# Hybrid encoder layer on one core: output block products with another order of splits and reads, row statistics on ScalarE, and an earlier sum for the last attention block

## The chip, the cores and the metric

The kernel runs on one core of a Trainium2 chip. The metric is the device time of one execution in microseconds (us), and the figure for a kernel is the median of several executions. "Faster" and "slower" mean a smaller and a larger median.

Five engines work side by side, each with a queue of its own that it takes strictly in order: PE (TensorE, the matrix multiplications), DVE (VectorE), ACT (ScalarE), POOL (GpSimd) and SP (SyncE, which here only issues DMAs). An engine waits when the next instruction in its queue needs a result of another engine or of a DMA; everything behind that instruction waits with it.

## The reference

One layer of a bidirectional encoder for 2048 tokens of width 1024, in float32. Two groups of heads work on the same input, their results stand side by side, one projection mixes them, and a LayerNorm closes the layer:

```python
def hybrid_mixer(x, positions, w_in, ..., w_out):
    h = x @ w_in
    (g_q, g_k, g_v, g_gate, g_lr_f, g_lr_b, m_cq, m_ckv, m_kr, m_gate) = jnp.split(h, idx, axis=-1)
    o_a = gla_branch(g_q, g_k, g_v, g_gate, g_lr_f, g_lr_b, ...)        # gated linear attention, width 512
    o_b = mla_branch(m_cq, m_ckv, m_kr, m_gate, positions, ...)         # latent attention, softmax, width 512
    return jnp.concatenate([o_a, o_b], axis=-1) @ w_out

def layer_norm(t, g, b):
    mu = jnp.mean(t, axis=-1, keepdims=True)
    var = jnp.mean(jnp.square(t - mu), axis=-1, keepdims=True)
    return (t - mu) * lax.rsqrt(var + LN_EPS) * g + b

x = layer_norm(DEEPNORM_ALPHA * x + mixed, ln_g, ln_b)
```

The change touches the end only: the last block of the softmax attention, the product with `w_out`, and the LayerNorm of its rows.

## The kernel before

**Stages.** Input projection and gated linear attention come first, then 16 blocks of softmax attention (one head and 512 queries each), then the product with `w_out`. The last two overlap; the stretch that matters here is the last 125 us of 1291.

**Precision by three matmuls.** Every float32 operand is split into a part `hi` (rounded, by ACT, line 392) and the rest `lo` (by POOL or DVE, line 398). One product is three matmuls, hi·hi, hi·lo and lo·hi, recorded at lines 446, 447 and 448 (`mm3`). So the matmul of line 448 is the first one that needs the `lo` part of the left operand.

**Output product, chunks 0 to 7.** The 2048 rows are 16 chunks of 128. Chunks 0 to 7 are multiplied directly: `product` or `part` issues 24 matmuls for each of the two halves of 512 columns. `residual` adds ALPHA times the input rows and takes row statistics of each half on DVE (`bn_stats`, line 2241). `finish_a` joins the statistics (line 2253 `mv`, line 2254 `u`), subtracts the mean and multiplies with `ln_g` (line 2256, two halves), and has ACT work out 1/sqrt in six small instructions (lines 2258 to 2263, `ln_l` to `ln_r`). `finish_b` multiplies with that and adds `ln_b` (line 2269, two halves on DVE), and SP writes the rows out (line 2270). `ln_psum` (line 2144) copies `ln_g` and `ln_b` into PSUM early in this stage.

**Output product, chunks 8 to 15.** Two chunks at a time form a `Pair` (line 1961), four pairs in all. Row 0 of pair p is chunk 9+2p, row 1 is chunk 8+2p. A pair is a 2x2 block product after Strassen and Winograd: seven products P1 to P7 of half size, 12 matmuls each, in place of eight. The left operands are A11, A12, A22 and the sums S1 to S4 (`add`, DVE line 2008). The seven products go in turn to four PSUM banks `pw0` to `pw3`, and each bank is used again within the pair and by the next pair. What empties the banks: ACT copies bank 0 twice (`c1`, `c7`, line 2033), DVE adds these copies into bank 2 (`U2`, `U3`, line 2036), and DVE reads the banks into the output rows (line 2042 for the first read of a half, line 2044 for later ones; R1, R5, R5b, R6, R2, R7 belong to row 0 or to both, R3, R4, R4b to row 1). The half rows get their statistics at line 2050.

**What feeds a pair.** `load` (line 1974) has SP fetch the two inputs of a chunk and its gates; `gate` (line 1996) has POOL multiply half of the chunk with two gates, two instructions for each chunk. The tiles that pairs 1 and 3 load into are named `lng` and `lnb` in the trace, since they are the slots that ln_g and ln_b came in; those of pairs 0 and 2 are named `of`.

**What sets the order.** In this last stage each instruction gets a place, a time in us: that of the pair plus a number of the table `PLACE_PAIR` (lines 140 to 148). All are sorted by place and `in_order` (line 408) ties them in that order on every engine. The numbers give an order alone; when a thing runs is decided by its waits.

**The last attention block.** Its row sums are turned and added by `tsum` (four small transposes on PE, `sx15`), then `rcp` on DVE (a reduction, line 1762, and a reciprocal, line 1766). `turn` transposes the reciprocals on PE (`rt`, line 1777), `y` multiplies the block with its value weights on PE (tile `y`), and `yc` copies that out on ACT (line 1806). The bank that `y` uses is the one that the first half of chunk 7 (`po7`) is written to next.

Of the kernel before, what the change touches and what calls it, by code (L numbers as in the profile page):

```python
# [9 lines left out]
F32 = mybir.dt.float32  # L10
# [133 lines left out]
    read=dict(c1=2.78, R1=5.99, R5=7.88, U2=10.61, R6=11.24, R5b=11.87, R2=12.5, bn12=13.13, c7=14.91, U3=15.63,  # L144
              R3=16.26, bn22=16.89, R7=17.52, bn11=18.15, R4=20.34, R4b=20.97, bn21=21.6, fa=(18.78, 22.23), fb=(23.79, 25.68)),
    read_last=dict(c1=2.78, R1=5.99, R5=7.88, U2=10.61, R6=11.24, R5b=11.87, R2=12.5, bn12=13.13, R7=13.7, bn11=14.3, c7=16.4,
                   U3=17.1, R3=17.7, bn22=17.8, R4b=17.71, fa=(14.9, 20.0), fb=(17.9, 24.0)),
# [234 lines left out]
class K:  # L382
# [1215 lines left out]
    def attention(self):  # L1598
# [4 lines left out]
        with ExitStack() as ctx:  # L1603
# [357 lines left out]
class Pair:  # L1961
# [76 lines left out]
    def read(self, r, n, ps, first, cs=slice(0, 512)):  # L2038
        o = self.rows[r]
        rr = o["rr"][:, n, cs]  # L2040
        if first:
            self.nc.vector.scalar_tensor_tensor(rr, o["xr"][:, n, cs], ALPHA, ps(), ALU.mult, ALU.add)
        else:
            self.nc.vector.tensor_tensor(rr, ps(), rr, ALU.add)
# [6 lines left out]

    def put(self, put, T, last):
# [23 lines left out]
        at(e["c7"], self.copy, bank[b["P7"]])  # L2076
        at(e["U3"], self.sum, bank[2])
        for n, r, h, x, first in (("R1", 0, 0, 0, True), ("R5", 1, 1, 1, True), ("R6", 0, 1, 3, True), ("R5b", 0, 1, 1, False),
                                  ("R2", 0, 1, 2, False), ("R3", 1, 1, 2, False), ("R7", 0, 0, b["P2"], False),
                                  ("R4b", 1, 0, 2, last)) + (() if last else (("R4", 1, 0, 3, True),)):  # L2080
            at(e[n], self.read, r, h, bank[x], first)
        at(e["bn12"], self.stats, 0, 1, 1)
        at(e["bn11"], self.stats, 0, 0, 0)
        if not last:
            at(e["bn22"], self.stats, 1, 1, 1)
            at(e["bn21"], self.stats, 1, 0, 0)
        else:
            at(e["bn22"], self.stats, 1, 1, 2, 3)
            for i, x in enumerate((3, 0)):
                cs, half = slice(256 * i, 256 * i + 256), lambda x=x: bank[x]()[:, :256]  # L2090
                at(t["P4"] + PAIR_US / 14 * i, self.product, "P4", half, cs)
                at(t["P4"] + PAIR_US / 14 * (i + 1) + 0.05, self.read, 1, 0, half, False, cs)
                at(t["P4"] + PAIR_US / 14 * (i + 1) + 0.06, self.stats, 1, 0, i, 3, cs)
        for r in range(2):
            at(e["fa"][r], op.finish_a, self.rows[r])
            at(e["fb"][r], op.finish_b, self.rows[r])


class OutProj:
# [147 lines left out]
    def finish_a(self, o):  # L2247
        kern, nc, sm = self.k, self.nc, self.sm
        V, Ac = nc.vector, nc.scalar
# [5 lines left out]
        for n in range(2):  # L2255
            V.scalar_tensor_tensor(rr[:, n], rr[:, n], mv[:, 0:1], self.ln[0][n], ALU.subtract, ALU.mult)
        l, y, t, w, rs = (sm.tile([P, 1], F32, tag=f"rs_{i}", name=f"ln{c}_{i}") for i in "lytwr")
# [8 lines left out]
    def finish_b(self, o):  # L2266
        kern, nc, c, rr = self.k, self.nc, o["c"], o["rr"]
        for n in range(2):
            nc.vector.scalar_tensor_tensor(rr[:, n], rr[:, n], o["rs"], self.ln[1][n], ALU.mult, ALU.add)
# [69 lines left out]
```

## Time and profile before

| what | value |
|---|---|
| median of three executions | 1294.27 us (1293.17, 1294.27, 1297.21) |
| the profiled execution, its own time | 1292.98 us |
| the profiled execution, its span in the trace | 1291.2 us |
| mean granted clock of TensorE | 0.994 |
| PE busy | 1258.6 us, 97% of the span |
| DVE busy | 955.1 us, 74% |
| ACT busy | 862.1 us, 67% |
| POOL busy | 845.4 us, 65% |
| chunk 7's last product ends, pair 0 begins | 1198.4 us |
| first matmul of pairs 1, 2 and 3 | 1221.9, 1240.9 and 1261.1 us |
| last matmul | 1280.3 us |

Times within the trace count from the start of the span. A row of the timeline gives the start, the duration, the engine, the line, the operation, the tile written and the tiles read, the shape, and in square brackets how long the engine had been idle before it and what it had waited for. Matmul starts are 0.227 us apart at the full clock for the usual 128x512 tile; the record's own duration is longer since matmuls overlap.

### The profile page before, as it was taken

To read this page: it belongs to the slowest core of one execution; us is meant where nothing else is said; L and a number is where in the kernel's file an instruction comes from. 1 tells how busy PE (TensorE), PEld (TensorE's weight loads), DVE (VectorE), ACT (ScalarE), POOL (GpSimd) and SP (SyncE) were. 2 spreads that over 40 slices of the span, in tenths; PEclk is the share of its full clock that TensorE was granted. 3 is DMA by queue.
4 is the path that set the end of the run, shared out by engine and by line. 5 is a ranking of instruction groups with operands and counts; after the bars stand their busy time and mean duration, and the time that the engine had idled before them with its cause. 6 is when DMAs were issued, how large, how long until landed. Compare 5 with 4: busy or idle time off the path is not lost.

```text
span 1291.2 us, 20146 instructions
## 1 busy us (share of the span) xinstructions
PE 1258.6 (97%) x6928; PEld 1112.4 (86%) x6928; DVE 955.1 (74%) x1722; ACT 862.1 (67%) x1520; POOL 845.4 (65%) x544
## 2 busy tenths in 40 slices
PE   7999999999999999999999999999999999999996
PEld 7999999999889999999788888888888888887775
DVE  6865775555675555555898888888888889468898
ACT  7765657666676556655688888888888888523432
POOL 0245555453567666671288888889999999946861
PEclk9999999999999999999999999999999999999998
DMA  8332525253665555565401111122223112368851
GB/s 296 96 93 62 181 69 171 82 156 98 221 218 182 189 193 180 196 213 167 135 1 41 42 41 41 42 58 66 58 79 101 42 41 103 127 217 321 284 196 65
DMA packets 122518, 166.81 MB, mean 129 GB/s; under 512 B 18502, under 2 KB 71118, under 8 KB 121776
## 3 DMA queue, kind: packets, MB, share of 16 engines
q1 hardware_dynamic: 114256, 163.39, 39.7%
q0 software_dynamic: 768, 2.10, 0.5%
q8 instruction: 55, 0.90, 0.3%
q10 hardware_dynamic: 7392, 0.03, 0.3%
q14 instruction: 47, 0.39, 0.2%
HBM read 106.72 MB, written 58.75 MB: 128 GB/s over the span
## 4 chain that ended last, share of the span: by engine, by line
PE 76%; DVE 6%; POOL 4%; DMA 3%; ACT 3%; issue 3%; SPq 1%; DVEq 0%; POOLq 0%; ACTq 0%
PE pS L1632 4%; PE pS L1634 4%; PE pS L1635 4%; PE pS L1633 4%; PE pS L1636 4%; PE o L446 4%; PE o L447 4%; PE o L448 4%; PE ipa L446 3%; PE ipa L448 3%; PE ipa L447 3%; PE pz L447 2%; PE pz L446 2%; PE pz L448 2%; PE ipg L446 2%
## 5 line engine op out<-in xcount | busy, mean ns | idle before, releaser
L398 POOL TENSOR_TENSOR pl<-s,ph 128x1024 fp32r<-128x1024 f32 x128 | 306.1, 2415 | 56.3 <-ACT ph L392 56.3
L1654 DVE TENSOR_TENSOR rm<-pS,rm 128x512 f32<-128x512 f32 x210 | 144.8, 689 | 26.2 <-ACT s L1641 20.6
L1678 DVE TENSOR_TENSOR s<-s,mb 128x1024 f32<-128x1024 f32 x128 | 151.2, 1213 | 9.4 <-PE mb L1672 9.3
L1641 ACT ACTIVATE s<-pS 128x1024 f32<-128x1024 f32 x128 | 131.2, 1025 | 37.5 <-PE pS L1636 33.4
L392 ACT ACTIVATE ph<-s 128x1024 fp32r<-128x1024 f32 x128 | 134.9, 1057 | 13.5 <-PE o L448 12.7
L1682 ACT ACTIVATE s<-s 128x1024 f32<-128x1024 f32 x128 | 131.5, 1051 | 13.4 <-DVE s L1678 13.3
L446 PE MATMUL ipa<-wah,xah 128*128 128x384 f32 (+1 forms) x384 | 130.5, 340 | 6.7 <-ACT wah L392 6.7
L1095 POOL TENSOR_TENSOR Us<-Us,cw 128x512 f32<-128x512 f32 x16 | 18.6, 1163 | 174.1 <-DVE Us L1093 158.6
L448 PE MATMUL ipa<-wah,xal 128*128 128x384 f32 (+1 forms) x384 | 125.3, 326 | 0.0
L447 PE MATMUL ipa<-wal,xah 128*128 128x384 f32 (+1 forms) x384 | 125.0, 326 | 0.0
L1632 PE MATMUL pS<-qh,ckvT_h 128*128 128x512 f32 x256 | 102.7, 401 | 0.8 <-DVE rm L1654 0.4
L446 PE MATMUL o<-ph,vh 128*128 128x512 f32 x256 | 101.2, 395 | 0.0
L1633 PE MATMUL pS<-ql,ckvT_h 128*128 128x512 f32 x256 | 99.9, 390 | 0.0
L1635 PE MATMUL pS<-rh,krs 128*128 128x512 f32 x256 | 99.9, 390 | 0.0
L1634 PE MATMUL pS<-qh,ckvT_l 128*128 128x512 f32 x256 | 99.9, 390 | 0.0
L448 PE MATMUL o<-ph,vl 128*128 128x512 f32 x256 | 99.9, 390 | 0.0
L1636 PE MATMUL pS<-rl,krs 128*128 128x512 f32 x256 | 99.9, 390 | 0.0
L447 PE MATMUL o<-pl,vh 128*128 128x512 f32 x256 | 99.8, 390 | 0.0
L1705 DVE TENSOR_TENSOR ap<-ap,s 128x512 f32<-128x512 f32 x120 | 83.1, 692 | 3.5 <-ACT s L1682 0.9
L446 PEld LDWEIGHTS ipa<-wah,xah 128*128 128x128 f32 x384 | 73.6, 192 | 7.2 <-ACT wah L392 6.7
L446 PE MATMUL pz<-xch,wzh 128*128 128x256 f32 x256 | 74.9, 293 | 0.0
L447 PEld LDWEIGHTS ipa<-wal,xah 128*128 128x128 f32 x384 | 73.6, 192 | 0.6 <-DVE wal L398 0.2
(433 smaller groups left out, 3901.0 us busy)
## 6 DMA issues: line engine op xcount, KB each, us to landing
xcf<-xT_dram SPq DMA_DIRECT2D x16, 512.0 KB, 5.1
xr<-x_dram SPq DMA_DIRECT2D x16, 512.0 KB, 6.3
xaf<-xT_dram SPq DMA_DIRECT2D x14, 512.0 KB, 3.9
wb<-wO_dram SPq DMA_DIRECT2D x16, 256.0 KB, 2.9
oib<-oi_s SPq DMA_DIRECT2D x16, 256.0 KB, 4.0
qdb<-qd_s SPq DMA_DIRECT2D x16, 256.0 KB, 4.4
SU<-su_s SPq DMA_DIRECT2D x16, 256.0 KB, 4.7
ub<-u_s SPq DMA_DIRECT2D x16, 256.0 KB, 4.2
```

Of the source, the lines that this page charges most:

```text
L392: return nc.scalar.activation(dst, src, AF.Copy).ins
L398: return e.tensor_tensor(dst, src, hi.bitcast(F32), ALU.subtract).ins
L446: mm(out, ah, bh, start=start, stop=False)
L447: mm(out, ah, bl, start=False, stop=False)
L448: mm(out, al, bh, start=False, stop=stop)
L1632: mm(ps[:, e], kh, qh, start=True, stop=False)
L1633: mm(ps[:, e], kh, ql, start=False, stop=False)
L1634: mm(ps[:, e], kl, qh, start=False, stop=False)
L1635: mm(ps[:, e], kr, rh, start=False, stop=False)
L1636: mm(ps[:, e], kr, rl, start=False, stop=True)
L1654: V.tensor_tensor(d["rm"], src[:, e], d["rm"], ALU.max)
L1678: V.tensor_tensor(s, s, d["mb"][:, None, :].to_broadcast([P, 2, QB]), ALU.subtract)
```

## The change

Five things, all in the last 125 us.

1. For the last attention block, `tsum` and `rcp` are issued before the product of chunk 5 and no longer after it.
2. On POOL the `lo` part of S4 of pair 0 moves up from the place 4.49 to -2.2, which is ahead of the gates of pair 1. Those gates get places of their own (`gate1`).
3. In pairs 0 to 2 the banks are read in another order: R5b directly after R5, R2 ahead of R6. Row 0 no longer gets its statistics from `bn_stats` on DVE but from ACT: `squares` sums the row by a copy of 128x1024 that accumulates, makes the negative mean `nm`, and squares the two halves with the mean taken off, accumulating again; `scale` makes the variance and runs the six instructions of 1/sqrt. On DVE `centre` subtracts the mean and multiplies with `ln_g` in one instruction of 128x1024. The places of `finish_a` and `finish_b` move. On SP the write of xr8 moves behind the four loads of chunk 15.
4. In the last pair the second copy (`c7`) and U3 are gone; DVE reads P7's bank itself for the two halves of row 1 that need it (R3p, R4p), two more reads. `copy_lnb` has ACT copy `ln_b` from PSUM to SBUF. Row 0 of the last pair is finished by ACT (scale) and POOL (add of that copy) in place of DVE (`finish_first`).
5. `ln` becomes a tile of 128x2x512 in place of a list of halves, and the 1/sqrt chain a function (`rsqrt`) of its own.

```diff
-    read=dict(c1=2.78, R1=5.99, R5=7.88, U2=10.61, R6=11.24, R5b=11.87, R2=12.5, bn12=13.13, c7=14.91, U3=15.63,
-              R3=16.26, bn22=16.89, R7=17.52, bn11=18.15, R4=20.34, R4b=20.97, bn21=21.6, fa=(18.78, 22.23), fb=(23.79, 25.68)),
-    read_last=dict(...),
+    gate1=((-14.6, -13.3), (-19.95, -18.6)),
+    read=dict(c1=2.78, R1=5.9, R5=6.5, R5b=7.1, U2=10.61, R2=11.24, R6=11.87, c7=14.91, U3=15.63, R3=16.26, bn22=16.89,
+              R7=17.52, sq=18.25, R4=20.34, R4b=20.97, bn21=21.6, rs=21.9, fa=(21.7, 22.23), fb=(23.9, 26.7)),
+    read_last=dict(c1=2.78, lnb=3.5, R1=5.0, R5=6.3, R5b=6.9, U2=8.9, R2=9.5, R3=10.1, R4b=10.7, R6=11.5, bn12=12.1,
+                   R7=14.1, bn11=14.7, R3p=16.9, R4p=17.5, bn22=18.1, fa=(15.3, 20.2), fb=(17.0, 20.3)),
...
+                    if c > 4:
+                        tsum(nb - 1)
+                        rcp(nb - 1)
                     op.product(rest[c])
                     op.finish(rest[c])
-                with self.after(*last.values()), fixed():
-                    for f in {4: (tot, oh, ol), 5: (tsum, rcp)}[c]:
-                        f(nb - 1)
+                if c == 4:
+                    with self.after(*last.values()), fixed():
+                        for f in (tot, oh, ol):
+                            f(nb - 1)
...
+    def squares(self, r):
+        Ac, o = self.nc.scalar, self.rows[r]
+        t, o["nm"] = self.small(o, "st"), self.small(o, "nm")
+        o["sq"] = [self.small(o, f"sq{n}") for n in range(2)]
+        Ac.activation(o["rr"], o["rr"], AF.Copy, accum_out=t)
+        Ac.activation(o["nm"], t, AF.Copy, scale=-1.0 / D)
+        for n, tag in enumerate(("wv_h", "wv_l")):
+            q = self.op.bp.tile([P, QB], F32, tag=tag, name=f"{tag}q{o["c"]}", bufs=1)
+            Ac.activation(q, o["rr"][:, n], AF.Square, bias=o["nm"], accum_out=o["sq"][n])
+
+    def scale(self, r):
+        Ac, o = self.nc.scalar, self.rows[r]
+        v, u = self.small(o, "v"), self.small(o, "u")
+        Ac.activation(v, o["sq"][1], AF.Copy, scale=1.0 / D, bias=LN_EPS)
+        Ac.activation(u, o["sq"][0], AF.Identity, scale=1.0 / D, bias=v)
+        self.op.rsqrt(o, u)
+
+    def centre(self, r):
+        o = self.rows[r]
+        self.nc.vector.scalar_tensor_tensor(o["rr"], o["rr"], o["nm"], self.op.ln[0], ALU.add, ALU.mult)
+
+    def copy_lnb(self):
+        self.lnb = self.op.bp.tile([P, 2, 512], F32, tag="pl", name="lnbc", bufs=3)
+        self.nc.scalar.activation(self.lnb, self.op.ln[1], AF.Copy)
+
+    def finish_first(self):
+        o, c = self.rows[0], self.c[0]
+        for n in range(2):
+            rr = o["rr"][:, n]
+            self.nc.scalar.activation(rr, rr, AF.Copy, scale=o["rs"])
+            self.nc.gpsimd.tensor_tensor(rr, rr, self.lnb[:, n], ALU.add)
+            self.nc.sync.dma_start(self.k.out[c * P:(c + 1) * P, n * 512:(n + 1) * 512], rr)
...
-                at(P_["gate"][r][n], self.gate, r, n)
+                at(P_["gate1" if self.p == 1 else "gate"][r][n], self.gate, r, n)
...
-            at(P_["lo"][n], self.lo, n)
+            at(-2.2 if n == "S4" and not self.p else P_["lo"][n], self.lo, n)
...
+        if last:
+            reads = (("R1", 0, 0, 0), ("R5", 1, 1, 1), ("R5b", 0, 1, 1), ("R2", 0, 1, 2), ("R3", 1, 1, 2), ("R4b", 1, 0, 2),
+                     ("R6", 0, 1, 3), ("R7", 0, 0, b["P2"]), ("R3p", 1, 1, b["P7"]), ("R4p", 1, 0, b["P7"]))
```

The table's numbers show little by themselves, so three places follow as the instructions stand in the queues.

**DVE, around the sums of the last attention block.** The row of line 1762 adds the sums (`sx`, from PE) and that of line 1766 takes their reciprocal. `rr_12919` is chunk 4, `rr_13042` and `rr_13050` are chunk 5. Before:

```order
L2253 BN_AGGR mv_12949<-bn_12920 128x2
L2254 TENSOR_SCALAR u_12950<-mv_12949 128x1
L2256 SCALAR_TENSOR_TENSOR rr_12919<-rr_12919,mv_12949,lng 128x512 x2
L2269 SCALAR_TENSOR_TENSOR rr_12919<-rr_12919,ln_r,lnb 128x512 x2
L398 TENSOR_TENSOR ofl_12974<-o_12437,ofh_12972 128x512
L2240 SCALAR_TENSOR_TENSOR rr_13042<-xr_12818,po_12993 128x512 x2
L2241 BN_STATS bn_13043<-rr_13042 128x6 x2
L1762 TENSOR_REDUCE rc_13074<-sx_13069 128x4
L2253 BN_AGGR mv_13048<-bn_13043 128x2
L1766 RECIPROCAL rc_13074<-rc_13074 128x4
```

With the change:

```order
L1763 TENSOR_REDUCE rc_12998<-sx_12993 128x4
L2308 BN_AGGR mv_12949<-bn_12920 128x2
L1767 RECIPROCAL rc_12998<-rc_12998 128x4
L2309 TENSOR_SCALAR u_12950<-mv_12949 128x1
L2311 SCALAR_TENSOR_TENSOR rr_12919<-rr_12919,mv_12949,lng 128x512 x2
L2328 SCALAR_TENSOR_TENSOR rr_12919<-rr_12919,ln_r,lnb 128x512 x2
L399 TENSOR_TENSOR ofl_12974<-o_12437,ofh_12972 128x512
L2295 SCALAR_TENSOR_TENSOR rr_13050<-xr_12818,po_13001 128x512 x2
```

The reduction and the reciprocal moved from behind chunk 5's statistics to ahead of chunk 4's finish. On PE the four transposes moved likewise, from behind chunk 5's 48 matmuls to ahead of them. (Line numbers of the changed kernel are higher by 1 at line 398 and by up to 60 further down.)

**POOL, between pair 0 and pair 1.** Line 398 makes `lo` parts, line 1996 applies gates; `lng` and `lnb` are the chunks of pair 1 here. Before:

```order
L398 TENSOR_TENSOR S2l_13228<-of_12988,S2h_13224 128x512
L1996 TENSOR_TENSOR lnb<-lnb,gr_12729 128x512
L398 TENSOR_TENSOR S3l_13264<-of_12888,S3h_13261 128x512
L1996 TENSOR_TENSOR lnb<-lnb,gr_12729 128x512
L1996 TENSOR_TENSOR lng<-lng,gr_12739 128x512 x2
L398 TENSOR_TENSOR A22l_13320<-of_12888,A22h_13268 128x512
L398 TENSOR_TENSOR A12l_13338<-of_12988,A12h_13259 128x512
L398 TENSOR_TENSOR S4l_13344<-of_12988,S4h_13266 128x512
L398 TENSOR_TENSOR A11l_13358<-lng,A11h_13322 128x512
```

With the change:

```order
L399 TENSOR_TENSOR S2l_13228<-of_12988,S2h_13224 128x512
L399 TENSOR_TENSOR S3l_13263<-of_12888,S3h_13260 128x512
L399 TENSOR_TENSOR S4l_13269<-of_12988,S4h_13265 128x512
L2001 TENSOR_TENSOR lnb<-lnb,gr_12729 128x512 x2
L399 TENSOR_TENSOR A22l_13320<-of_12888,A22h_13267 128x512
L399 TENSOR_TENSOR A12l_13338<-of_12988,A12h_13258 128x512
L2001 TENSOR_TENSOR lng<-lng,gr_12739 128x512 x2
L399 TENSOR_TENSOR A11l_13359<-lng,A11h_13322 128x512
```

S4's `lo` part of pair 0 now stands ahead of six instructions that it stood behind: the four gates of pair 1, A22l and A12l. The number of instructions up to A11l of pair 1 is the same.

**DVE, where the last pair begins.** `xr_13589` is row 0 of pair 2 (chunk 13), `xr_13612` row 1 (chunk 12), `xr_13783` and `xr_13806` are the rows of the last pair (chunks 15 and 14). With the change:

```order
L2081 SCALAR_TENSOR_TENSOR xr_13589<-xr_13589,nm_13855,ln_13112 128x1024
L2308 BN_AGGR mv_13913<-bn_13851 128x2
L2309 TENSOR_SCALAR u_13914<-mv_13913 128x1
L2311 SCALAR_TENSOR_TENSOR xr_13612<-xr_13612,mv_13913,ln_13112 128x512 x2
L2328 SCALAR_TENSOR_TENSOR xr_13589<-xr_13589,ln_r,ln_13115 128x512 x2
L2048 SCALAR_TENSOR_TENSOR xr_13783<-xr_13783,pw_13272 128x512
L2048 SCALAR_TENSOR_TENSOR xr_13806<-xr_13806,pw_13273 128x512
L2048 SCALAR_TENSOR_TENSOR xr_13783<-xr_13783,pw_13273 128x512
L2328 SCALAR_TENSOR_TENSOR xr_13612<-xr_13612,ln_r,ln_13115 128x512 x2
L2041 TENSOR_TENSOR pw_13274<-pw_13274,pc_13894 128x512
L2050 TENSOR_TENSOR xr_13783<-pw_13274,xr_13783 128x512
L2050 TENSOR_TENSOR xr_13806<-pw_13274,xr_13806 128x512
```

The finish of chunk 13 (line 2328, first of the two) stands ahead of all reads of the last pair, as it did before; the centring ahead of it is one instruction, and after it three first reads stand together. On ACT, `lnbc` (the copy of `ln_b`) stands behind the 1/sqrt chains of chunks 13 and 12, and in the program the finish of chunk 13 waits for it, since both read the same PSUM tile.

More of the change, by code (lines that the diff above doesn't have):

```diff
@@ L2075, in put @@
         at(e["U2"], self.sum, bank[2])
[L2076 to L2083, printed above, removed]
+        if last:
+            reads = (("R1", 0, 0, 0), ("R5", 1, 1, 1), ("R5b", 0, 1, 1), ("R2", 0, 1, 2), ("R3", 1, 1, 2), ("R4b", 1, 0, 2),
+                     ("R6", 0, 1, 3), ("R7", 0, 0, b["P2"]), ("R3p", 1, 1, b["P7"]), ("R4p", 1, 0, b["P7"]))
+        else:
+            at(e["c7"], self.copy, bank[b["P7"]])
+            at(e["U3"], self.sum, bank[2])
+            reads = (("R1", 0, 0, 0), ("R5", 1, 1, 1), ("R5b", 0, 1, 1), ("R2", 0, 1, 2), ("R6", 0, 1, 3), ("R3", 1, 1, 2),
+                     ("R7", 0, 0, b["P2"]), ("R4", 1, 0, 3), ("R4b", 1, 0, 2))
+        for n, r, h, x in reads:
+            at(e[n], self.read, r, h, bank[x])
         if not last:
@@ L2135, in load_ln @@
             self.nc.sync.dma_start(t, self.k.ins[n].rearrange("p (a d) -> p a d", a=2))
-        self.ln = [[t[:, n] for n in range(2)] for t in self.ln_sb]
+        self.ln = list(self.ln_sb)
     def pair_banks(self):
@@ L2144, in ln_psum @@
         self.nc.scalar.activation(t, self.ln_sb[w], AF.Copy)
-        self.ln[w] = [t[:, n] for n in range(2)]
+        self.ln[w] = t
     def fetch_t(self, n):
```

52 lines of the change are left out of this document (33 added, 19 removed).

## The prediction

> **What bounds the kernel now.** I read the share of busy time first (PE 97%), then PE's own waits in the last 190 us, since whatever PE does not wait for cannot be won there. The view of waits, from 1100 us on (engine, line, releaser: total us, times, longest):
>
> ```profile
> PE rt L1777 <- DVE u L2254: 2.6, 1, 2.6
> PE pw L448 <- POOL S4l L398: 2.5, 1, 2.5
> PE pw L446 <- DVE xr L2044: 0.8, 1, 0.8
> ```
>
> Three stalls, and the change aims at all of them. What a stall really costs is in the windows (PE, PEld, DVE, ACT, POOL busy, then granted clock, DMA share, GB/s):
>
> ```profile
> 1210.00:1214.00 4.00, 4.00 (x12) 3.17 (x11) 2.90 (x3) 1.33 (x3) 2.71 (x3) 0.59 1.07 364
> 1240.00:1260.00 20.00, 19.19 (x85) 15.57 (x84) 19.45 (x32) 8.05 (x21) 12.69 (x11) 1.00 0.38 143
> ```
>
> After the 2.5-us stall the clock is 0.59 for one stretch; after the 0.8-us stall (1255.5) it stays 1.00. The second row also shows DVE as good as full (19.45 of 20) while PE has 0.8 to spare: in the pairs DVE paces. Now PE's timeline at the first stall and at the pairs' first matmuls:
>
> ```profile
> 1176.74 0.39 PE L448 MATMUL pmb<-woh,ol 128*128 128x512 f32 x1
> 1179.68 0.27 PE L1777 MATMUL rt<-ident,rc 128*4 128x128 f32 x1 [2.56 <-DVE u L2254]
> 1180.87 0.63 PE L446 MATMUL px<-woh,oh 128*128 128x512 f32 x1
> 1183.42 0.41 PE L446 MATMUL px<-woh,oh 128*128 128x512 f32 x1
> 1187.53 0.39 PE L446 MATMUL po<-woh,oh 128*128 128x512 f32 x1
> 1198.41 0.39 PE L446 MATMUL pw<-woh,A11h 128*128 128x512 f32 x1
> 1221.86 0.39 PE L446 MATMUL pw<-woh,A11h 128*128 128x512 f32 x1
> 1240.90 0.39 PE L446 MATMUL pw<-woh,A11h 128*128 128x512 f32 x1
> 1261.07 0.39 PE L446 MATMUL pw<-woh,A11h 128*128 128x512 f32 x1
> ```
>
> From 1180.87 to 1183.42 six matmuls take 2.55 us, 0.425 each against 0.227 later: with `rt` and `y` about eight slow ones, some 1.6 us on top of 2.56. A pair without a stall takes 84 matmuls, 84 x 0.227 = 19.05 us (pair 1: 1240.90 - 1221.86 = 19.04). Pair 0 took 23.45, 4.4 too much: 2.5 waiting, 1.9 slow. Pair 2 took 20.17, 1.1 too much.
>
> The Trainium skill, "TensorE: Matmul & The Clock Gate", Part 1, has it that the clock drops after at least one idle window of about 3.4 us and that the slow stretch lasts as long. Here idle times of 2.46 and 2.56 us sufficed, and the slow stretch agrees (1180.0 to 1183.4). By that number neither stall would have slowed PE, and taking away the one at S4l would win 2.5 us where the rows give 4.4; the rows decide.
>
> **First part: the sums one chunk sooner.** `rt` waits for DVE's reciprocal, which stands behind chunk 5's statistics:
>
> ```profile
> 1178.65 0.67 DVE L1762 TENSOR_REDUCE rc<-sx 128x4 f32<-128x512 f32 x1
> 1179.36 0.18 DVE L1766 RECIPROCAL rc<-rc 128x4 f32<-128x4 f32 x1
> 1185.46 0.63 ACT L392 ACTIVATE A11h<-of 128x512 fp32r<-128x512 f32 x1 [1.92 <-DMA of<-oa_s]
> 1186.15 0.57 ACT L1806 ACTIVATE yc<-y 128x512 f32<-128x512 f32 x1
> ```
>
> Placed ahead of chunk 4's finish the reciprocal is done some 9 us earlier, so `rt` follows at 1177.1 without a wait: 2.56 + 1.6 = 4.2 us off this place. But the next thing behind is `po`, which writes the bank that `yc` copies out, and `yc` stands on ACT behind A11h, which waits for its input until 1185.46. `yc` ends at 1186.72 whatever PE does. PE, ready at 1187.53 - 4.2 = 1183.3, would idle to 1186.8: 3.5 us, longer than the two stalls that dropped the clock, so another 1.6 us slow. Pair 0 then starts at 1198.41 - 0.73 + 1.6 = 1199.25, 0.85 later than before; without a clock drop 0.75 sooner. I take the drop. So this part by itself wins nothing; it swaps one stall for another.
>
> **Second part: S4's lo part.** POOL and the wait's other end:
>
> ```profile
> 1198.50 0.63 ACT L392 ACTIVATE S4h<-of 128x512 fp32r<-128x512 f32 x1 [1.15 <-DVE of L2008]
> 1199.82 1.29 POOL L398 TENSOR_TENSOR S3l<-of,S3h 128x512 fp32r<-128x512 f32 x1
> 1207.89 1.71 POOL L398 TENSOR_TENSOR S4l<-of,S4h 128x512 fp32r<-128x512 f32 x1
> 1216.93 1.29 POOL L1996 TENSOR_TENSOR of<-of,gr 128x512 f32<-128x512 f32 x1 [2.27 <-DMA of<-ob_s]
> 1225.81 1.31 POOL L398 TENSOR_TENSOR S4l<-lng,S4h 128x512 fp32r<-128x512 f32 x1
> ```
>
> S4h is there at 1199.1. In the new order POOL makes S4l right behind S3l, which no longer waits for a gate: done near 1200.5 instead of 1209.6, while P3 of pair 0 asks for it at 1199.25 + 8.16 + 0.45 = 1207.9. Stall and slow stretch go: -4.4. What it is moved past (four gates, A22l, A12l) has slack: at 1.27 us each A12l is done near 1205.5, wanted at 1212.9; pair 1's A11l ends near 1209.3, as before. SP's next load waits for A22l, but also stands behind a write that sets its time (the write of chunk 7), so it is not moved. Pair 1 starts at 1199.25 + 19.05 = 1218.3 instead of 1221.86: -3.56.
>
> **What is late next.** The gates of pair 2 stand on POOL ahead of pair 1's S4l. The gate at 1216.93 waited for a DMA, and from it on POOL works without a gap: S4l of pair 1 ends at 1227.1, as before. P3 of pair 1 now asks for it at 1218.3 + 8.61 = 1226.9. A wait of 0.2: the pace has reached the transfer. This is a floor: pair 2 cannot start before 1237.6 (before: 1240.90, so -3.3), and it hardly matters whether pair 0 came 0.85 later or 0.75 sooner.
>
> **Third part: DVE relieved in the pairs.** The first read after the old pair's centring, three pairs in a row, and ahead of the last one the end of a pair:
>
> ```profile
> 1222.43 0.68 DVE L2042 SCALAR_TENSOR_TENSOR xr<-xr,pw 128x512 f32<-128x512 f32 x1
> ...
> 1242.61 0.68 DVE L2042 SCALAR_TENSOR_TENSOR xr<-xr,pw 128x512 f32<-128x512 f32 x1
> ...
> 1260.15 0.69 DVE L2050 BATCH_NORM_STATS2 bn<-xr 128x6 f32<-128x512 f32 x1
> 1260.88 0.21 DVE L2253 BATCH_NORM_AGGREGATE mv<-bn 128x2 f32<-128x12 f32 x1
> 1261.12 0.15 DVE L2254 TENSOR_SCALAR u<-mv 128x1 f32<-128x1 f32 x1
> 1261.19 1.40 DVE L2256 SCALAR_TENSOR_TENSOR xr<-xr,mv,ln 128x512 f32<-128x512 f32 x2
> 1262.51 0.68 DVE L2042 SCALAR_TENSOR_TENSOR xr<-xr,pw 128x512 f32<-128x512 f32 x1
> ```
>
> From read to read (1222.43, 1242.61, 1262.51) DVE needs 20.2 and 19.9 us. Two `bn_stats` (0.73 to the next start here, some 0.61 elsewhere) and row 0's `mv` and `u` (0.24, 0.07) go: -1.65. What moves to ACT, and a wider form on DVE, have these nearest rows:
>
> ```profile
> L1678 DVE TENSOR_TENSOR s<-s,mb 128x1024 f32<-128x1024 f32 x128 | 151.2, 1213 | 9.4 <-PE mb L1672 9.3
> L1682 ACT ACTIVATE s<-s 128x1024 f32<-128x1024 f32 x128 | 131.5, 1051 | 13.4 <-DVE s L1678 13.3
> L1379 ACT ACTIVATION_READ_ACCUMULATOR sqm<-ipm x16: 186/194/195, 376.3 to 592.8; 128x1 f32 x16
> L1540 ACT ACTIVATE og<-Ob x16: 578/595/599, 381.3 to 586.5; 128x512 f32<-128x512 f32 x16
> 1276.80 0.20 ACT L2258 ACTIVATE ln_l<-u 128x1 f32<-128x1 f32 x1 [10.04 <-DVE u L2254]
> 1278.36 0.58 ACT L2033 ACTIVATE pc<-pw 128x512 f32<-128x512 f32 x1
> ```
>
> Centring in one instruction of 1024 instead of two of 512 is not in the trace: between 1.21 (line 1678) and the 1.40 of the two together, I take -0.1. DVE then needs 18.2 a pair, less than PE's 19.05, and R5b right behind R5 frees bank 1 early: pair 2's stall of 0.81 and its slow neighbours go, -1.1. Pair 3 starts at 1237.6 + 19.05 = 1256.65: -4.4 against 1261.07.
>
> ACT, busy 8.05 us of 20, gets a copy of 1024 (1.05), two squares of 512 (0.60), an accumulator read each (0.19), and three instructions of one column (0.2 to 0.3): 3.6 us a pair, with accumulation bounded from below by nothing and from above by a second pass (+2.2). The last two rows hold the six instructions of a 1/sqrt chain: 1278.36 - 1276.80 = 1.6. All of it is hidden as long as the 1/sqrt of row 0 reaches DVE in time. It stands behind `c1`, the copy of the new pair's P1: 2.72 + 0.8 + 0.57 + 1.6 = 5.6 us into the pair. DVE waits for it some 0.4 us, and after its finish, reads and sums it releases R6's bank at about 15.2, with P4 due at 16.32: 1.1 us of cover.
>
> **Fourth part: the last pair.** The rows of its end:
>
> ```profile
> 1266.30 1.40 DVE L2269 SCALAR_TENSOR_TENSOR xr<-xr,ln_r,ln 128x512 f32<-128x512 f32 x2
> 1278.97 0.70 DVE L2036 TENSOR_TENSOR pw<-pw,pc 128x512 f32<-128x512 f32 x1 [0.89 <-ACT pc L2033]
> 1284.98 0.15 DVE L2254 TENSOR_SCALAR u<-mv 128x1 f32<-128x1 f32 x1
> 1286.85 1.41 DVE L2269 SCALAR_TENSOR_TENSOR xr<-xr,ln_r,ln 128x512 f32<-128x512 f32 x2 [0.41 <-ACT ln_r L2263]
> ```
>
> Before, the last finish starts 1286.85 - 1261.07 = 25.78 us into the pair, and the span ends 4.35 later. With the change the copy, U3 (0.73 and its wait of 0.89) and row 0's last finish (1.3) leave DVE, two reads (1.2) come. Against that stands a new wait: chunk 13's finish waits for `lnbc`, and that stands on ACT behind `c1` (3.5 us into the pair), v and u (0.57), two chains (1.6 each) and lasts 1.05 like the copies of 1024 above: 8.2 us in, while DVE is free near 5.2. Everything of the pair on DVE is behind it. From there: finish 1.32, three reads 1.80, finish 1.32, U2 0.73, three reads 1.83, R6 with statistics 1.32, R7 with statistics 1.44, `mv`, `u` 0.31, centring 1.31, two reads 1.22, statistics 0.65, two quarter reads with statistics 1.79, `mv` 0.28: 15.3, so `u` at 23.5 and, 1.87 later as before, the last finish at 25.4: -0.4. Row 0's end on ACT and POOL is over near 23 and not last.
>
> The Trainium skill, "PSUM — Partial Sum Buffer", section on bank collisions, says that two engines, readers too, may not touch one bank at once and are to be guarded by bank. That is this wait: both instructions only read `ln_b`. No row of this trace shows a price for it; without it the end would come some 2.3 us sooner.
>
> **The sum.** -4.4 (pair 3's start) - 0.4 (tail) = -4.8. The profiled execution took 1292.98 around a span of 1291.2: 1288.2. It lies 1.29 under the median shown, so on the median 1294.27 - 4.8 = 1289.5.
>
> **The rivals.**
>
> (A) Better than forecast: the wait for `lnbc` costs nothing, because ACT runs its chains before DVE is free: -7.1, 1287.2. For it: the old chains ran within 1.6 us. Against it: six instructions each in a row, behind `c1`. By 15%.
>
> (B) Given back: the transfers of pair 2's inputs land later still, for the DMA share is 1.07 there. At 2.3 us more, PE waits 2.5 us in pair 1 and the clock drops again: -4.8 + 2.3 + 1.65 = -0.9, 1293.4; half of that 1291.5. For it: there is a wait on them already. Against it: SP issues them no later than before. By 21%.
>
> (C) Slower: ACT's longer chain becomes the pace. Row 0's finish stands ahead of all reads of the next pair on DVE; if the statistics come x later than 5.6 us into the pair, P4 stalls by x - 1.1, three times. Even at x = 2.7 the gain is gone (3 x 1.6 = 4.8); at x = 3.5 the stalls of 2.4 drop the clock and each costs 4.0: -4.8 + 12 = +7.2, 1301.5. For it: two accumulating forms whose size the trace has only smaller (128x256). Against it: 3.5 us is as much as the whole added work. By 12%.
>
> **How the numbers follow.** Forecast 52%, its own range 1287.8 to 1291 (pair 2's floor gives or takes 1, the tail 1). A measurement here tells 0.3% from no change, 3.9 us: 1290.4 to 1298.2 is "same". The forecast's 52% lies mostly under 1290.4 (47), with (A) 15: faster 0.62. Same: 5 of the forecast, (B) 20: 0.25. (C) and a little of (B): slower 0.13. The range 1285.8 to 1294.3 reaches over (A), the forecast and (B), and leaves out (C) and the edge of (A).
>
> **What will show it.** No wait of PE for S4l of pair 0, and pair 0 in 19.05 us. `rt` without a wait, but `po` waiting about 3.5 us for `yc`, then a slow stretch. P3 of pair 1 waiting little for POOL. No wait at P2 of pair 2, DVE under 19 us a pair. A DVE gap of about 3 us before chunk 13's finish, released by ACT. I am wrong if `po` does not wait, if PE waits over 1 us in pair 1, or if DVE's finish of chunks 9 or 11 waits over 1.5 us for ACT.

## The result, and the profile after

| | before | with the change |
|---|---|---|
| median | 1294.11 us (11 runs, 1292.26 to 1297.21) | 1290.3 us (11 runs, 1287.88 to 1292.85) |
| ratio | | 0.9969, 95% interval 0.9958 to 0.9979 |
| the profiled execution, its own time | 1292.98 us | 1290.68 us |
| its span in the trace | 1291.2 us | 1288.9 us |

The change makes the kernel faster by 3.8 us, 0.31%. The two profiled executions are only 2.3 us apart, since that of before was among its faster ones; sums within the traces are held against the 2.3.

First PE's three longest waits after 1100 us in the changed kernel, in the form of the prediction's first fence:

```profile
PE po L447 <- ACT yc L1807: 3.4, 1, 3.4
PE pw L447 <- DVE xr L2048: 0.4, 1, 0.4
PE pw L449 <- POOL S4l L399: 0.4, 1, 0.4
```

The three old stalls (2.6, 2.5 and 0.8 us) are gone, and one of 3.4 has come. The timeline of PE shows where, and when the pairs begin (start, duration, engine, line, tiles, wait):

```profile
1187.39 0.62 PE L447 MATMUL po<-woh,oh 128*128 128x512 f32 x1 [3.42 <-ACT yc L1807]
1200.03 0.39 PE L447 MATMUL pw<-woh,A11h 128*128 128x512 f32 x1
1219.07 0.39 PE L447 MATMUL pw<-woh,A11h 128*128 128x512 f32 x1
1228.24 0.50 PE L449 MATMUL pw<-woh,S4l 128*128 128x512 f32 x1 [0.40 <-POOL S4l L399]
1238.80 0.39 PE L447 MATMUL pw<-woh,A11h 128*128 128x512 f32 x1
1258.13 0.39 PE L447 MATMUL pw<-woh,A11h 128*128 128x512 f32 x1
```

The reader is to see three things. Chunk 7's 48 matmuls take 1200.03 - 1187.39 = 12.64 us instead of 48 x 0.227 = 10.9, so 1.7 us are slow after the new stall. Pair 0 takes 19.04, the bare product. Pairs 1 and 2 take 19.73 and 19.33, and a little is lost in each. Set against before, the starts of pairs 0 to 3 moved by +1.6, -2.8, -2.1 and -2.9 us. (Some 0.5 us of lateness is already there at 1160 us, ahead of all changed instructions.)

DVE's timeline in the pairs and at the end of the changed kernel:

```profile
1234.78 1.76 DVE L2013 TENSOR_TENSOR of<-of 128x512 f32<-128x512 f32 x1
1242.20 1.28 DVE L2081 SCALAR_TENSOR_TENSOR xr<-xr,nm,ln 128x1024 f32<-128x1024 f32 x1 [0.96 <-ACT wv_lq L2070]
1245.30 1.41 DVE L2328 SCALAR_TENSOR_TENSOR xr<-xr,ln_r,ln 128x512 f32<-128x512 f32 x2 [0.20 <-ACT ln_r L2322]
1267.54 1.40 DVE L2328 SCALAR_TENSOR_TENSOR xr<-xr,ln_r,ln 128x512 f32<-128x512 f32 x2 [2.14 <-ACT lnbc L2085]
1284.53 1.41 DVE L2328 SCALAR_TENSOR_TENSOR xr<-xr,ln_r,ln 128x512 f32<-128x512 f32 x2 [0.41 <-ACT ln_r L2322]
```

DVE now waits for ScalarE at the turn of every pair (0.48, 0.96 and 0.96 us for the squares, and 0.2 each for the first two of the 1/sqrt) and once for 2.14 us, for the copy of `ln_b`, at the start of the last pair. The last finish starts 1284.53 - 1258.13 = 26.40 us into the last pair, against 25.78 before: the tail became 0.6 us longer. So the whole gain in the trace, 2.3, is pair 3's earlier start of 2.9 less 0.6.

### The profile page after: what moved, and what is told of

Its sections match the earlier page's. It is cut to its first block, busy times and chain, and to the rows that moved or that the text cites. A ratio compares the mean times of both kernels' runs of the same rounds, so it can differ in the third digit from the quotient of the medians.

```text
span 1288.9 us, 20174 instructions
## 1 busy us (share of the span) xinstructions
PE 1257.7 (98%) x6928; PEld 1109.6 (86%) x6928; DVE 949.8 (74%) x1706; ACT 873.8 (68%) x1549; POOL 847.7 (66%) x546
## 4 chain that ended last, share of the span: by engine, by line
PE 75%; DVE 6%; ACT 5%; DMA 4%; POOL 3%; issue 2%; SPq 0%; DVEq 0%; POOLq 0%; ACTq 0%
PE o L447 4%; PE o L448 4%; PE o L449 4%; PE pS L1633 4%; PE pS L1634 4%; PE pS L1635 4%; PE pS L1636 4%; PE pS L1637 4%; PE ipa L447 3%; PE ipa L449 3%; PE ipa L448 3%; PE pz L448 2%; PE pz L449 2%; PE pz L447 2%; PE ipg L447 2%
```

## The experiments

Each was timed against the kernel before on the same chip. The chips differ between groups of experiments, and the median of before on them between 1294.1 and 1295.3 us, so two experiments are best compared by their ratios. Where the text speaks of a start or a wait, it is that of the experiment's own profile.

### One part at a time, and all but one

**e1: the sums alone.** The kernel before, with this edit:

```diff
+                    if c > 4:
+                        tsum(nb - 1)
+                        rcp(nb - 1)
                     op.product(rest[c])
```

> The kernel before with the first part alone (sums of the last attention block a chunk sooner). Theory (the stall moves to po7, which waits for yc15; DVE then paces the pairs): rt waits for nothing, po7 waits about 3.5 us for yc15 and the clock drops after it; pair 0 starts 0.8 to 1.6 us later than before's 1198.4; the wait for S4l of pair 0 shrinks from 2.5 to about 1.5 us and drops no clock; the end moves by -0.6 to +0.3 us. Rival 1 (the removed stall is a gain of its own): -4.2 us. Rival 2 (the new stall adds to the others): +0.8 us or more.

Measured: 1294.52 against 1294.39 us, ratio 0.9999 (0.9990 to 1.0008). PE's waits:

```profile
PE po L446 <- ACT yc L1806: 3.0, 1, 3.0
PE pw L448 <- POOL S4l L398: 2.3, 1, 2.3
PE pw L446 <- DVE xr L2048: 0.8, 1, 0.8
```

`rt` waits no longer, `po` waits 3.0 for `yc`, and pairs 1, 2 and 3 start at 1221.90, 1240.96 and 1261.07: to 0.06 us where they were. The theory holds for the end. It missed the middle: pair 0 came only 0.26 us later, so the wait for S4l was still 2.3, the clock dropped after it, and pair 0 took 23.2 us.

**e2: S4's lo part alone.** The kernel before, with the second part:

```diff
-            at(P_["lo"][n], self.lo, n)
+            at(-2.2 if n == "S4" and not self.p else P_["lo"][n], self.lo, n)
```

together with `gate1`.

> The kernel before with the second part alone (lo of S4 of pair 0 ahead of pair 1's gates). Theory (DVE paces from 1210.9 us on, where it waits for POOL's A11l of pair 1): the 2.5-us wait and the slow stretch go and pair 1 starts about 4.4 us sooner, but PE gives most of it back in new waits for DVE's reads in pairs 1 and 2; pair 3 starts only 0.6 to 1.2 us sooner and the time falls by 0.6 to 1.2 us. Rival (the parts add up): pair 3 and the end 3.5 to 4.4 us sooner.

Measured: 1293.8 us, ratio 0.9991 (0.9982 to 0.9999). PE waits for the freeing of bank 1 in pairs 0, 1 (0.58 us) and 2; its timeline shows the first and the last, and the windows around the first (columns as in the prediction) show the clock:

```profile
1214.08 0.50 PE L447 MATMUL pw<-woh,A12h 128*128 128x512 f32 x1 [3.27 <-DVE xr L2045]
1254.01 0.50 PE L447 MATMUL pw<-woh,A12h 128*128 128x512 f32 x1 [0.66 <-DVE xr L2045]
```

```profile
1212.00:1214.00 2.00, 0.00 (x0) 0.00 (x0) 1.97 (x4) 1.87 (x4) 1.16 (x1) 1.00 1.08 360
1214.00:1216.00 2.00, 1.93 (x8) 1.61 (x9) 1.93 (x5) 0.28 (x1) 0.12 (x1) 1.00 1.08 282
```

The wait for POOL is gone, and in the same pair PE waits 3.27 us for DVE to free bank 1. Nearly the whole gain is given back 5 us later, as the theory said, but already in pair 0 and not first in pairs 1 and 2. That stall dropped no clock, and neither did the one of 2.92 us at `rt`, so that pair 0 began 1.36 us sooner than before; that is chance, for the edit touches only later instructions. From the first matmul of pair 0 to that of pair 3 it took 62.57 us, against 62.66 before.

**e3: the reads and the statistics on ScalarE alone.** The kernel before with the third part; the last pair keeps its copy, U3 and DVE finish.

> The kernel before with the third part alone (order of reads and row 0's statistics on ScalarE in pairs 0 to 2; last pair as before). Theory (PE's stall at S4l paces up to pair 1, so a lighter DVE wins only the later 0.8-us stall and what hangs on it): pairs 1 and 2 start as before (1221.9 and 1240.9), pair 3 1.1 us sooner, the end 0.5 to 1.1 us sooner. Rival (DVE's relief of 1.65 us a pair shows in full): 3 to 5 us sooner. Rival 2 (ScalarE's chain paces): DVE's finish of chunks 9 and 11 waits over 1.5 us, no gain or slower.

Measured: 1293.95 us, ratio 0.9993 (0.9984 to 1.0001). PE still waits for S4l, longer even:

```profile
1210.04 0.62 PE L448 MATMUL pw<-woh,S4l 128*128 128x512 f32 x1 [3.61 <-POOL S4l L398]
```

Pairs 1 to 3 start at 1222.2, 1241.3 and 1261.0. A lighter DVE wins nothing while POOL holds PE: pair 0's first matmul to pair 3's takes 63.32 us.

**e4: all but the sums.** The changed kernel with `tsum` and `rcp` back behind chunk 5.

> The changed kernel without the first part (sums where they stood before). Theory (floor by pair 1's S4l on POOL, which the landing of pair 2's inputs sets): rt waits 2.6 us again, po7 not at all, pair 0 starts 0.5 to 1 us sooner than in the changed kernel, PE then waits for S4l of pair 1 about 1 us instead of 0.4, and pair 2 and the end are within 0.5 us of the changed kernel (about 1290). Rival (the first part is worth what it removes): 4 us slower than the changed kernel.

Measured: 1290.77 us, ratio 0.9972 (0.9960 to 0.9983); the change itself has 0.9969. PE's waits:

```profile
PE rt L1778 <- DVE u L2305: 3.7, 1, 3.7
PE pw L449 <- POOL S4l L399: 0.8, 1, 0.8
PE pw L447 <- DVE xr L2044: 0.4, 1, 0.4
```

Pair 0 started at 1198.84 instead of 1200.03, and pair 1's wait for S4l doubled. The first part is worth nothing here, as the theory said.

**e5: all but the last pair's part.** The changed kernel with the last pair of before.

> The changed kernel with the last pair as it was before (no copy of ln_b, row 0 finished on DVE, bank 1 copied and added). Theory (what the last pair saves on DVE is eaten by the wait for lnbc): pairs start as in the changed kernel; chunk 13's finish waits for its own 1/sqrt, until about 7.3 us into the pair instead of 9.4, and the last finish starts 26 to 26.7 us into the pair, against 26.4 in the changed kernel: same time within 0.5 us. Rival (the last pair's part is worth its saved work): 1.5 to 2.5 us slower than the changed kernel.

Measured: 1290.37 us, ratio 0.9966 (0.9954 to 0.9978). Pair 3 starts at 1257.82 and the last finish at 1284.16, 26.34 us later. The last pair's part as written wins nothing.

So each of the first three parts by itself moves the time by at most 0.1%, and without the first, or without the last pair's part, the full gain stays. That leaves the second and third part together. They were not run as a pair without the rest, but e1 and e5 differ by just these two (and the form of `ln`): ratio 0.9999 and 0.9966, and 62.40 and 58.70 us from pair 0's first matmul to pair 3's. With one of the two this stretch takes 62.57 (e2) or 63.32 us (e3), with both 58.10 in the change and 58.51 in e4. S4's lo part lets PE go (e2), and a DVE that frees bank 1 early lets it keep going (in e2 it did not).

### The waits that are left

**e6: the copy of ln_b early.** The changed kernel with

```diff
-    read_last=dict(c1=2.78, lnb=3.5, ...
+    read_last=dict(c1=2.78, lnb=-1.0, ...
```

> The changed kernel with the copy of ln_b ahead of the row statistics of chunk 13 on ScalarE instead of behind two 1/sqrt chains. Theory (that copy is what chunk 13's finish waits for, and everything of the last pair on DVE is behind it): DVE's wait of 2.1 us falls below 0.4, the last finish starts about 24.3 us into the last pair, the time falls by 1.7 to 2.1 us against the changed kernel. Rival 1 (the tail is set by the products): the wait moves to the reads of banks, gain under 0.5 us. Rival 2 (the copy in its new place delays the statistics by its 1 us): gain about 1 us.

Measured: 1287.74 us, ratio 0.9941 (0.9929 to 0.9954), 2.6 us below the change by the medians. Pair 3's first matmul and the last finish:

```profile
1256.73 0.39 PE L447 MATMUL pw<-woh,A11h 128*128 128x512 f32 x1
```

```profile
1280.90 1.41 DVE L2328 SCALAR_TENSOR_TENSOR xr<-xr,ln_r,ln 128x512 f32<-128x512 f32 x2 [0.41 <-ACT ln_r L2322]
```

The finish starts 24.17 us into the pair instead of 26.40. The wait for `lnbc` was on the path in full, and its 2.2 us are what the spacing in the trace shows. By the ratios the gain is 0.28%, 3.6 us; the profile also has pairs 2 and 3 starting 1.4 us sooner than in the change, and pair 2's start lies ahead of anything that the edit touches (taken up below).

**e7: row 1's centring first.** The changed kernel with `fa=(22.3, 21.7)` in place of `fa=(21.7, 22.23)`.

> The changed kernel with row 1's mean and centring ahead of row 0's centring on DVE in pairs 0 to 2, so that DVE works while ScalarE squares; row 1's 1/sqrt chain then stands ahead of row 0's on ScalarE. Theory (ScalarE's chain from the last read of row 0 to its 1/sqrt paces DVE): DVE's waits for the squares (2.4 us in all) go and come back as longer waits for row 0's 1/sqrt, the finish of chunks 9 and 11 starts 1 to 1.5 us later, PE waits for DVE's reads in pairs 1 to 3; time 1 to 3 us above the changed kernel. Rival (DVE's own work paces): 1 to 2 us faster.

Measured: 1292.99 us, ratio 0.9990 (0.9981 to 0.9998), 2.7 us above the change. DVE's waits:

```profile
DVE xr L2328 <- ACT ln_r L2322: 5.8, 3, 2.7
DVE xr L2328 <- ACT lnbc L2085: 2.7, 1, 2.7
```

The waits for the squares went and came back as two of 2.7 for the 1/sqrt; the last pair starts at 1262.6. DVE's queue stands behind ScalarE's chain, wherever the wait is put. PE pays with waits of 1.6 us for S4l in pair 1 and 2.2 us ahead of P4 in pair 2.

**e8: four moves.** The changed kernel with

```diff
-    ... fa=(21.7, 22.23), fb=(23.9, 26.7)),
-    read_last=dict(c1=2.78, lnb=3.5, ...
+    ... fa=(22.3, 21.7), fb=(26.7, 26.45)),
+    read_last=dict(c1=2.78, lnb=-1.0, ...
-            at(-2.2 if n == "S4" and not self.p else P_["lo"][n], self.lo, n)
+            at(-2.2 if n == "S4" and self.p < 2 else P_["lo"][n], self.lo, n)
```

> The changed kernel with four moves: ln_b's copy early, row 1's centring ahead of row 0's, the first three reads of the next pair ahead of both finishes and row 1's finish ahead of row 0's, and S4l of pair 1 ahead of two of pair 2's gates on POOL. Theory (ScalarE's chain, the copy and POOL's order are the three paces left): no wait of PE for S4l of pair 1 (-0.4), DVE's waits for ScalarE under 0.5 us in each pair, no wait of PE in pairs 1 to 3, last finish about 23.5 us into the last pair: 3 to 4 us below the changed kernel, near 1286.5. Rival (the transfers of inputs set the pairs): pairs start as in the changed kernel and only the tail's 2 us are won.

Measured: 1287.59 us, ratio 0.9939 (0.9927 to 0.9951): the same as e6 within the noise, where 3 to 4 us below the change were expected. Pairs 0 and 1 take 19.04 us each, but pair 2 takes 19.69, and DVE's first read in it waits:

```profile
1243.88 1.88 DVE L2048 SCALAR_TENSOR_TENSOR xr<-xr,pw 128x512 f32<-128x512 f32 x3 [0.58 <-ACT pc L2038]
```

`c1` had come behind a 1/sqrt chain on ScalarE, and DVE does not read bank 0 until that copy is over.

**e10: that copy first.** e8 with `fa=(22.3, 21.85)`.

> The kernel of e8 with the copy of P1 ahead of row 1's 1/sqrt chain on ScalarE. Theory (in e8 that copy came late, so the next first read and a product waited for it): the 0.6-us wait of DVE and the 0.4-us wait of PE for pc go, pairs 1 and 2 take 19.04 us each, last finish 23.5 us into the last pair: 0.3 to 0.7 us below e8. Rival: row 1's finish waits for its later 1/sqrt instead, same time as e8.

Measured: 1285.92 us, ratio 0.9940 (0.9924 to 0.9955). The profile is of an execution of 1290.76 us, the longest of this kernel. Its `po` starts 5.0 us later than in e8, and another 1 us went in a longer slow stretch behind it; so only spacings are read:

```profile
1204.97 0.39 PE L447 MATMUL pw<-woh,A11h 128*128 128x512 f32 x1
1224.01 0.39 PE L447 MATMUL pw<-woh,A11h 128*128 128x512 f32 x1
1243.05 0.39 PE L447 MATMUL pw<-woh,A11h 128*128 128x512 f32 x1
1262.09 0.39 PE L447 MATMUL pw<-woh,A11h 128*128 128x512 f32 x1
```

Three pairs of exactly 19.04 us: nothing is lost in them any more. The last finish starts 22.5 us into the last pair. Whether the time is below e8 the intervals do not tell.

**e9: yc15 ahead of A11h.** The changed kernel with

```diff
-            at(P_["hi"][n], self.hi, n)
+            at(-15.2 if n == "A11" and not self.p else P_["hi"][n], self.hi, n)
```

> The changed kernel with the copy of the last attention block (yc15) ahead of pair 0's A11h on ScalarE, so that po7 waits for no load. Theory (the stall at po7 is not on the path; pair 0's fourth product and pair 1's S4l wait for POOL and transfers): po7 waits under 0.5 us, the clock holds, pair 0 starts 4 to 5 us sooner than 1200.0, but its P4 then waits 3 to 4 us for DVE's read R6, which stands behind the sum that waits for POOL's A11l; pair 1 starts at most 1 us sooner, the time falls by 0 to 1 us against the changed kernel. Rival (the stall is on the path): 4 to 5 us faster.

Measured: 1291.36 us, ratio 0.9977 (0.9968 to 0.9985), no better than the change. PE's timeline at the start of pair 0 and at its last product P4:

```profile
1193.94 0.39 PE L447 MATMUL pw<-woh,A11h 128*128 128x512 f32 x1
...
1213.55 0.76 PE L447 MATMUL pw<-woh,A22h 128*128 128x512 f32 x1 [3.12 <-ACT pc L2038]
```

and DVE's row ahead of R6, with the double read that ends with R6:

```profile
1209.56 1.75 DVE L2013 TENSOR_TENSOR lng<-s,lng 128x512 f32<-128x512 f32 x1 [1.18 <-POOL A11l L399]
...
1211.96 1.49 DVE L2050 TENSOR_TENSOR xr<-pw,xr 128x512 f32<-128x512 f32 x2
```

Pair 0 starts 6 us sooner and P4 waits 3.1 and then runs slow; pair 1 starts at 1218.80 against 1219.07. The profile names ScalarE's copy (over at 1213.50), but in the program P4 waits for R6, which ended at 1211.96 + 1.49 = 1213.45. Two candidates that end together are told apart by the program's waits, not by the profile.

**e11: e10 with yc15 first.**

> The kernel of e10 with yc15 ahead of A11h as in e9. Theory: po7 waits under 0.5 us, pair 0 starts 4 to 5 us sooner, P4 of pair 0 waits 3 to 4 us for DVE's R6 (behind the sum that waits for POOL's A11l of pair 1) and the clock drops after it; pair 1 starts within 1 us of e10's, same time within 0.7 us. Rival (with S4l early on POOL nothing else holds the pairs): 3 us or more below e10.

Measured: 1285.75 us, ratio 0.9930 (0.9917 to 0.9942). P4 of pair 0 waits 3.3 us, pair 1 starts at 1219.18. The same time as e10, as the theory said.

**e12: and the sum behind R6.** e11 with S2 of pair 1 and its two parts at -6.9, -6.8 and -6.7, so that R6 no longer stands behind the sum that waits for POOL.

> The kernel of e11 with that sum (S2 of pair 1, with its two parts) behind R6 of pair 0 on DVE. Theory (the sum's wait for POOL is what holds R6, and so P4 of pair 0): P4 waits under 1.5 us, for the weights loaded meanwhile or not at all, pair 1 starts 2 to 4 us sooner than in e10, the time falls by 1.5 to 3.5 us against e10. Rival (the inputs of pair 2 or DVE's work set the later pairs): pair 1 starts sooner, pairs 2 and 3 as in e10.

Measured: 1285.61 us (1283.73 to 1289.73), ratio 0.9936 (0.9920 to 0.9952). Pair 0 starts at 1193.06, its P4 waits 0.34, and pair 1 starts at 1213.3. Then pair 1's P4 stalls:

```profile
1232.41 0.47 PE L447 MATMUL pw<-woh,A22h 128*128 128x512 f32 x1 [2.00 <-ACT pc L2038]
```

6 us gained at pair 1 have become 3.0 at pair 3 (1254.31 against 1257.31 in e11), and by the medians nothing is left that can be told from noise. DVE's rows show what was late:

```profile
1213.10 0.69 DVE L2013 TENSOR_TENSOR lng<-lng 128x512 f32<-128x512 f32 x1 [2.07 <-POOL S2l L399]
...
1230.77 1.49 DVE L2050 TENSOR_TENSOR xr<-pw,xr 128x512 f32<-128x512 f32 x2
```

Pair 1's P4 needs DVE's R6, the end of the second row, 1230.77 + 1.49 = 1232.26; again ScalarE's copy ended just after it (1232.31). The move took away DVE's wait of 1.2 us for POOL's A11l, but it put the sum S4 directly behind S2, and there S4 waits 2.07 us for POOL's S2l, which it does not in e11. From there to R6 DVE worked without another wait. From one R6 to the next (1210.23 to 1232.26) DVE took 22.0 us, where PE needs 19.04. So DVE is late next once more. Another order was not tried. The kernels e10 to e12 are some 0.65% faster than before, and their order among each other is open.

## Why the prediction was right, and where its terms were off

**The sum.** Forecast 1289.5 us and -4.8, measured 1290.3 and -3.8, inside the range; in the traces -2.3. The term of pair 3's start was -4.4 and measured -2.9, the term of the tail -0.4 and measured +0.6. So the total came closer than its two terms did, and these are read from one execution each.

**First part: right, in mechanism and size.** The stall was to move to `po` with 3.5 us and 1.6 slow; measured 3.42 and 1.7. That the size fits so well is in part luck: in the experiments that keep both this part and the place of `yc`, the stall ran from 2.24 (e7) to 3.84 us (e6). That it wins nothing is shown by e1 and e4. What the length of a stall has to do with the clock is taken up in the last section.

**Second part: right.** Pair 0 in 19.05 (measured 19.04). That it wins next to nothing by itself, because DVE is late next, was not spelled out in the prediction's working; e2 shows it.

**What is late next: the mechanism right, the small wait partly luck.** Pair 1's wait for S4l was put at 0.2 and measured 0.40. But the gate ahead of it ran at 1218.00, where the prediction kept the 1216.93 of before, and pair 1 itself began 0.8 us later than forecast; in the wait the two nearly cancel. In pair 2's start they do not: 1238.80 instead of 1237.6. That is 1.2 of the 1.5 us by which pair 3 missed its forecast of 1256.65; the other 0.3 is pair 2's length. The floor is real: e4 and e5, whose pair 0 began a microsecond sooner, waited 0.8 and 1.1 there, and in both, as in the change, pair 2 began 20.8 us after that gate. But the gate's own time scatters. In the change, and in e6, whose edit touches only what comes later:

```profile
1218.00 1.30 POOL L2001 TENSOR_TENSOR of<-of,gr 128x512 f32<-128x512 f32 x1 [2.50 <-DMA of<-ob_s]
1216.52 1.30 POOL L2001 TENSOR_TENSOR of<-of,gr 128x512 f32<-128x512 f32 x1 [2.55 <-DMA of<-ob_s]
```

In e6 PE did not wait for S4l, and pair 3 began at 1256.73, where the prediction had put it. So the first term was missed in the change's own trace mainly by when one transfer landed; whether the change itself moves that landing is not shown.

**Third part: nearly right for PE, wrong for DVE's pace.** On PE pair 2 was to lose 1.1 us and lost 0.84 (20.17 to 19.33). DVE was to need 18.2 us a pair and wait 0.4 for ScalarE. From first read to first read it took 20.4 and 20.3 (the first of these with other waits in it, 1.2 of them for POOL's A11l; the second is compared here):

```profile
1205.89 1.88 DVE L2048 SCALAR_TENSOR_TENSOR xr<-xr,pw 128x512 f32<-128x512 f32 x3
...
1226.32 1.88 DVE L2048 SCALAR_TENSOR_TENSOR xr<-xr,pw 128x512 f32<-128x512 f32 x3
...
1246.62 1.88 DVE L2048 SCALAR_TENSOR_TENSOR xr<-xr,pw 128x512 f32<-128x512 f32 x3
```

Two terms were missing. First, I counted ScalarE's statistics as hidden up to the 1/sqrt, but the centring writes in place and waits until both squares have read the row. ScalarE's rows in the changed kernel:

```profile
1239.22 1.06 ACT L2066 ACTIVATE xr<-xr 128x1024 f32<-128x1024 f32 x1 [1.50 <-DVE xr L2050]
1240.19 0.18 ACT L2066 ACTIVATION_READ_ACCUMULATOR xr<-xr 128x1 f32 x1
1240.40 0.20 ACT L2067 ACTIVATE nm<-st 128x1 f32<-128x1 f32 x1
1240.64 0.73 ACT L2070 ACTIVATE wv_hq<-xr,nm 128x512 f32<-128x512 f32 x1
1241.36 0.71 ACT L2070 ACTIVATE wv_lq<-xr,nm 128x512 f32<-128x512 f32 x1
```

The added work is 2.9 us up to the last square, near what I summed (squares 0.72 each instead of 0.60), but DVE has only 2.0 us of other work meanwhile and waits 0.96. Second, the sum of S4 (line 2013) takes 1.76 in pairs 1 and 2 where before it took 0.95 and 0.68: in its new place it runs beside POOL's instructions, while the same sum in pair 0, with POOL idle, took 0.69. With these two, 1.2 of waiting and 0.8 to 1.1 of slower sums, the 1.65 saved are gone; what remains is the order of the reads. PE's wait of 0.81 for R5b in pair 2 did go. Its R6 is late by some 0.2 in pair 2, where I had given 1.1 of cover. The sign that the prediction named, DVE under 19 us a pair, did not come.

**The tail: the mechanism right, the place 1.2 us off.** `lnbc` was to end 8.2 us into the last pair; it ended at 9.4. ScalarE's squares of chunk 13 stand ahead of everything that I counted from:

```profile
1259.52 1.06 ACT L2066 ACTIVATE xr<-xr 128x1024 f32<-128x1024 f32 x1 [1.50 <-DVE xr L2050]
...
1262.37 0.58 ACT L2038 ACTIVATE pc<-pw 128x512 f32<-128x512 f32 x1
...
1266.50 1.01 ACT L2085 ACTIVATE lnbc<-ln 128x1024 f32<-128x1024 f32 x1
```

`c1` starts at 1262.37, 4.2 us into the pair and not 2.9, because it stands behind them, and they could only begin 1.4 us into the pair, when DVE's last read of that row was done. So DVE's pace, the miss of the third part, is paid here. DVE itself was free for the finish 7.3 us into the pair (1265.40) and not at 5.2, so the gap ahead of it was 2.14 us instead of the 3 named. All that follows on DVE is 1 us later, and so is the end. The sum from there (17.2 forecast, 1284.53 - 1267.54 = 17.0) was right.

**The rivals.** (A) fell: in e6 the wait is gone and the tail 2.2 us shorter, where the prediction had 2.3 as its price. (B) did not come about, though half of its mechanism did (in this execution the landing was 1.1 us later and the wait 0.2 longer). (C) is there in small: ScalarE's chain holds DVE up, by at most 1.2 us a pair; e7 brought it out in full, with waits of 2.7 and the gain of the change nearly gone.

## What to carry to other kernels

When several engines are nearly full, a removed stall is worth only the distance to the next engine that is late: work out that one before adding up gains, and expect parts that win nothing alone to win together (here 0.01%, 0.09% and 0.07% alone, each within 0.1% either way, and 0.31% together; the stretch of pairs 0 to 2 shows it better, with at most 0.3 us won by any one part and 4.6 by all). Moving work to an idle engine is free in busy time and not in latency: count from the last input to the result that the old engine waits for, with everything that stands ahead in the new engine's queue, and mind writes in place that wait for the new reader. A small copy at the wrong place in a queue can cost as much as it was made to save (here 2.2 us); look for who waits for it at the next use of what it reads.

## What the runs showed of the hardware

After idle times of TensorE the clock dropped or did not, and the length alone did not decide. Stalls of 2.24 us at `po` and 2.18 us ahead of P4 (both e7) dropped it; those of 2.92 us at `rt` and 3.27 us at A12h (both e2) left it at 1.00. The windows of the first:

```profile
1184.00:1186.00 2.00, 0.45 (x2) 0.03 (x1) 1.92 (x3) 0.66 (x3) 1.70 (x2) 1.00 0.84 277
1186.00:1188.00 2.00, 1.31 (x3) 1.12 (x4) 1.97 (x4) 0.64 (x3) 0.00 (x0) 0.62 0.60 183
1188.00:1190.00 2.00, 2.00 (x6) 1.52 (x6) 1.93 (x6) 1.44 (x5) 0.00 (x0) 0.53 1.05 341
```

The Trainium skill, "TensorE: Matmul & The Clock Gate", Part 1, has it that the clock drops after at least one idle window of about 3.4 us; the drops after 2.18 to 2.56 us do not agree with that. The same section of the Trainium skill also says that the window runs freely; a stall that covers most of one such window and one that lies across two could differ in this way. Which phase each stall met was not measured, so this is not shown. The slow stretches last 2.8 to 3.9 us here, two of them longer (5.3 us in e10, 5.8 in e9). Stalls of 0.8, 1.6 and 2.0 us (before, e7, e12) dropped nothing. A stall between 2.2 and 3.3 us thus costs its length and in most of these traces another 1.5 to 1.9 us, in e9 and e10 2.8 to 3.0.
